# The output projection of a hybrid transformer layer in a seven-product form, with x added by accumulating transfers and two plain pairs ahead of the first MLP product

## The chip, the cores and the metric

One NeuronCore of one Trainium2 chip. The metric is the device time of one launch in microseconds. Names of engines as in the profile: PE is TensorE (matmuls; PEld its weight loads), DVE VectorE, ACT ScalarE, POOL GpSimd, SP SyncE, which only issues transfers. Transfers that add to what lies at their destination ("accumulating") are issued by POOL in this kernel.

## The reference, cut to what matters

x has 512 tokens of 2048 features in float32, the hidden layer of the MLP 8192.

```python
def reference(x, g_mix, w_in, ..., w_oa, w_ob, w_out, g_ff, w_ff1, w_ff2):
    h = rms_norm(x, g_mix)
    q, k, v, u, v_sg, gate_a, gate_b = split(h @ w_in)
    y_a = stick_breaking_attention(q, k, v) @ w_oa
    y_b = spatial_gating(gelu(u), gelu(v_sg)) @ w_ob
    merged = sigmoid(gate_a) * y_a + sigmoid(gate_b) * y_b
    x = x + merged @ w_out
    h2 = rms_norm(x, g_ff)
    return x + square(relu(h2 @ w_ff1)) @ w_ff2
```

## The kernel before

Tokens are four blocks of 128 (`NTB`), features 16 tiles of 128 (`KT`), column pieces 512 wide (`W`). Every large product is made from float32 in three matmuls: each factor is split into a high part, rounded by ACT, and a low part, the difference made by DVE (`split_to`, L113 and L114), and `mm3` multiplies high by high, high by low and low by high (L72, L73, L74). `weight` (L99 and L101) does the same for a piece of a weight that SP loaded, 1024 elements to a partition; the split pieces go through a ring of six tiles, that is three pairs.

The stages in order of time: the input projection and attention; y_a (`by_column` over w_oa), y_b (`by_column` over w_ob) and merged (L836 on DVE, L847 on POOL); x + merged @ w_out; the first MLP product; the second MLP product. In w_out `by_token` goes over four column pieces j, and in each over eight pieces of two row tiles, with four banks of PSUM, one for each token block. x is loaded by SP into the tile `x2`, and when a column piece is done, `evac_x` adds the bank to it on DVE (L868), squares it on ACT for the norm (L869) and writes it to `kept`, from which it is added again at the end (L1086). In the steps of the next column piece `turned` transposes x2 on PE (L884), multiplies by gain and norm on DVE (L888) and splits the result, the factors of the first MLP product.

The MLP products use a form with seven products of half size in place of eight (`NAMES`: y11, y21, m7, m6, y22, m4, m5); sums and differences of the quarters are the factors (`factor`, L251, for activations, `Sums` for weights). The first MLP product has 32 pairs of hidden tiles; the first one (`PLAIN`) is made without that form by `plain_pair`, while the factors m7, m6, m5, m4 of the input are made, the other 31 by `strassen_pair`. The second one goes over eight blocks of `strassen_tokens`, each with seven products of two units (i = 0, 1) of 12 matmuls. `Sums` holds six raw tiles for each unit: the quarters w11, w12, w21, w22, and two sums. `a` = w11 + w21 is the factor of m7, `c` = a + w22 that of m6; then c becomes c + w12, the factor of y22; w21 gets w22 added by an accumulating transfer of POOL (L188) for m5.

The order on each engine is set by a scheduler with a timing model of its own, within the order of the data. Each engine, POOL among them, then takes its instructions strictly in that order. What is run beside the matmuls is queued in `behind`, one entry for each `step()`; `at_steps` puts functions at numbered steps (`steps[n]`), counted from the start of w_oa: w_oa has 0 to 15, w_ob 16 to 31. Raw tiles come from pools: a block's transfer into a tile waits until the block before has read it.

Of the kernel before, what the change touches and what calls it, by code (L numbers as in the profile page):

```python
# [35 lines left out]
def tile_hybrid_layer(ctx: ExitStack, tc: tile.TileContext, x, g_mix, w_in, g_q, g_k, ln_g, ln_b,  # L36
# [816 lines left out]

    EARLY = 6

    def first_factors(k):
        for name, sign, pool in (("m7", -1.0, long if k < LONG - KT // 2 else slots), ("m6", None, slots)):
            factor(hs, x2T[2 * k:2 * k + 2], k, name, sign, pool)
# [4 lines left out]
    kept = dram.tile([NTB, D // W, P, W], F32, name="kept")
    ss2 = const.tile([P, NTB, 4], F32, name="ss2")
    for j in range(D // W):
        def evac_x(tb, o):
# [1 line left out]
            nc.vector.tensor_tensor(out=t, in0=o, in1=t, op=ALU.add)  # L868
            nc.scalar.activation(out=o, in_=t, func=AF.Square, accum_out=ss2[:, tb, j:j + 1])  # L869
# [11 lines left out]
        def turned(c, j=j):  # L881
            t = aux("x2T")
            for tb in range(NTB):
                nc.tensor.transpose(out=t[:, tb * P:(tb + 1) * P], in_=x2[tb, j][:, c * P:(c + 1) * P],  # L884
                                    identity=ident)
            k = j * 4 + c
            keep = slot("x2T")
            nc.vector.scalar_tensor_tensor(out=keep, in0=t, scalar=gT2[:, k:k + 1], in1=rstd_b,  # L888
                                           op0=ALU.mult, op1=ALU.mult)
            x2T.append(keep)  # L890
            for half in range(2):
                name = "y" + "12"[k % 2] + "12"[half]
                hs[name, k // 2] = halves(keep[:, half * HS:(half + 1) * HS],
                                          long if name == "y11" else slots)

        behind.extend([lambda c=c, turned=turned: turned(c) for c in range(4)])
        if j == D // W - 2:
            behind.extend([lambda k=k: (first_factors(k), first_factors(k + 1)) for k in range(0, EARLY, 2)])
    flush()
# [220 lines left out]
```

## Time and profile before

| what | us |
|---|---|
| median of 3 runs (lowest, highest) | 2416.53 (2415.04, 2416.75) |
| the profiled execution's own time | 2416.75 |
| its span | 2415.0 |
| w_oa and w_ob, 795.0 to 984.4 | 189.4 |
| w_out, 984.4 to 1164.6 | 180.2 |
| the plain pair, 1164.6 to 1190.2 | 25.6 |
| five Strassen pairs, 1258.3 to 1355.2 | 96.9 |

In rows of a timeline the first number is the start, the second the length, in us. In groups the count stands behind x, then the busy time in us and the mean of one in ns, then the idle time of the engine ahead of them with what ended it. Matmuls are pipelined, so that a row's length is more than the interval between two; the interval is taken from the starts of rows a known number of matmuls apart.

### The profile page before, as it was taken

The numbers are of one execution on the slowest core, as the hardware profiler recorded it, in microseconds if no ns is written. First come the engines' busy times: TensorE is split into PE (matmuls) and PEld (weight loads), VectorE is DVE, ScalarE is ACT, GpSimd is POOL, SyncE is SP. The second block draws the span as 40 slices with busy tenths as digits, with TensorE's granted clock in tenths as the row PEclk, the third lists the DMA queues.
The fourth block names the chain that finished last, engine by engine and source line by source line (L and its number), as shares of the span: only waits on it lengthen the run. The fifth ranks groups of instructions, "written<-read, shape, count | busy, mean of one in ns | idle before, by whom it ended". The sixth has DMA issues, their size and how long they took to land.

```text
span 2415.0 us, 34398 instructions
## 1 busy us (share of the span) xinstructions
PE 2401.7 (99%) x12452; PEld 2058.2 (85%) x12452; DVE 1879.3 (78%) x2555; ACT 1283.5 (53%) x1977; POOL 475.0 (20%) x586
## 2 busy tenths in 40 slices
PE   9999999999999999999999999999999999999999
PEld 8888888888888878888988888888888788888887
DVE  5576887777778554445788888888888898989987
ACT  5335666666666323233577777777765443333333
POOL 0101222222223322100000000000025334322210
PEclk9999999999999999999999999999999999999999
DMA  5557887878888843443488888888887999877753
GB/s 184 196 161 162 170 176 173 187 170 180 174 180 194 329 149 131 131 148 125 102 229 225 239 232 232 225 231 232 226 271 262 315 274 323 252 219 210 233 183 96
DMA packets 511770, 490.94 MB, mean 203 GB/s; under 512 B 20657, under 2 KB 401649, under 8 KB 511601
## 3 DMA queue, kind: packets, MB, share of 16 engines
q1 hardware_dynamic: 385232, 336.68, 43.7%
q0 software_dynamic: 126080, 151.55, 29.8%
q8 instruction: 98, 1.61, 0.3%
q10 hardware_dynamic: 288, 0.52, 0.1%
q14 instruction: 72, 0.58, 0.1%
HBM read 397.97 MB, written 89.65 MB: 202 GB/s over the span
## 4 chain that ended last, share of the span: by engine, by line
PE 94%; DMA 2%; DVE 2%; ACT 1%; issue 1%; POOL 0%; SPq 0%; DVEq 0%; ACTq 0%
PE q L223 18%; PE fork L223 13%; PE q L226 9%; PE q L73 7%; PE q L74 7%; PE q L72 7%; PE fork L226 7%; PE xo L72 2%; PE xo L74 2%; PE xo L73 2%; DMA w_raw<-in_w_ff_dram 1%; PE v L72 1%; PE v L73 1%; PE v L74 1%; PE vg L72 1%; PE vg L73 1%
## 5 line engine op out<-in xcount | busy, mean ns | idle before, releaser
L113 ACT CAST w_hi<-w_raw 128x1024 fp32r<-128x1024 f32 (+1 forms) x639 | 671.3, 1051 | 726.1 <-PE q L73 325.5
L114 DVE TENSOR_TENSOR w_lo<-w_raw,w_hi 128x1024 fp32r<-128x1024 f32 (+1 forms) x639 | 777.8, 1218 | 181.8 <-ACT w_hi L113 166.0
L223 PE MATMUL q<-ys,w_hi 128*128 128x512 f32 x1664 | 419.0, 393 | 1.7 <-ACT fork L231 1.7
L73 PE MATMUL q<-w_lo,ys 128*128 128x512 f32 x896 | 349.3, 390 | 2.7 <-DVE w_lo L114 2.5
L74 PE MATMUL q<-w_hi,ys 128*128 128x512 f32 x896 | 348.7, 389 | 0.0
L223 PEld LDWEIGHTS q<-ys,w_hi 128*128 128x128 f32 x1664 | 299.4, 189 | 56.1 <-ACT fork L231 2.1
L72 PE MATMUL q<-w_hi,ys 128*128 128x512 f32 x896 | 312.8, 389 | 0.2 <-DVE total L1062 0.2
L188 POOL DMA_DIRECT2D w_raw<-in_w_ff_dram x58 | 80.9, 1395 | 892.8 <-ACT act L1000 230.9
L223 PE MATMUL fork<-ys,w_hi 128*128 128x512 f32 x968 | 242.2, 392 | 0.0
L226 PEld LDWEIGHTS q<-ys,w_lo 128*128 128x128 f32 x1664 | 225.2, 190 | 14.3
L226 PE MATMUL q<-ys,w_lo 128*128 128x256 f32 x1664 | 232.1, 282 | 0.0
L101 DVE TENSOR_TENSOR w_lo<-w_raw,w_hi 128x1024 fp32r<-128x1024 f32 x99 | 124.8, 1260 | 136.4 <-ACT w_hi L99 131.5
L99 ACT CAST w_hi<-w_raw 128x1024 fp32r<-128x1024 f32 x99 | 104.1, 1051 | 227.5 <-issue 95.6
L223 PEld LDWEIGHTS fork<-ys,w_hi 128*128 128x128 f32 x968 | 175.9, 189 | 32.6
L73 PEld LDWEIGHTS q<-w_lo,ys 128*128 128x128 f32 x896 | 168.2, 188 | 40.1 <-DVE w_lo L114 5.2
L72 PEld LDWEIGHTS q<-w_hi,ys 128*128 128x128 f32 x896 | 168.1, 188 | 35.6 <-issue 0.6
L74 PEld LDWEIGHTS q<-w_hi,ys 128*128 128x128 f32 x896 | 168.2, 188 | 34.7
L1008 POOL DMA_DIRECT2D ys<-store x224 | 126.7, 578 | 182.1 <-PE q L74 115.9
L226 PEld LDWEIGHTS fork<-ys,w_lo 128*128 128x128 f32 x968 | 132.0, 190 | 9.4
L186 DVE TENSOR_TENSOR w_raw<-w_raw 128x1024 f32<-128x1024 f32 x91 | 111.1, 1222 | 31.3 <-DVE act L285 12.1
L1062 DVE SCALAR_TENSOR_TENSOR total<-q,plus,total 128x512 f32<-128x512 f32 x180 | 132.0, 744 | 4.2 <-PE q L74 4.1
L226 PE MATMUL fork<-ys,w_lo 128*128 128x256 f32 x968 | 135.0, 282 | 0.0
(263 smaller groups left out, 3887.0 us busy)
## 6 DMA issues: line engine op xcount, KB each, us to landing
w_raw<-in_w_ff_dram SPq DMA_DIRECT2D x256, 512.0 KB, 5.7
w_raw<-in_w_in_dram SPq DMA_DIRECT2D x143, 512.0 KB, 5.4
ys<-store POOLq DMA_DIRECT2D x224, 256.0 KB, 6.5
w_raw<-in_w_ff_dram POOLq DMA_DIRECT2D x58, 512.0 KB, 6.9
w_raw<-in_w_in_dram POOLq DMA_DIRECT2D x56, 512.0 KB, 6.5
store<-ys_hi SPq DMA_DIRECT2D x90, 256.0 KB, 5.3
store<-ys_lo SPq DMA_DIRECT2D x90, 256.0 KB, 5.2
w_raw<-in_w_out_dram SPq DMA_DIRECT2D x32, 512.0 KB, 4.1
```

Source lines behind the costliest of these rows:

```text
L72: nc.tensor.matmul(o, lhsT=lh[0], rhs=rh[0], start=start, stop=False, **kw)
L73: nc.tensor.matmul(o, lhsT=lh[0], rhs=rh[1], start=False, stop=False, **kw)
L74: nc.tensor.matmul(o, lhsT=lh[1], rhs=rh[0], start=False, stop=stop, **kw)
L99: nc.scalar.copy(out=hi, in_=raw)
L101: nc.vector.tensor_tensor(out=lo, in0=raw, in1=f32(hi), op=ALU.subtract)
L113: nc.scalar.copy(out=hi, in_=src)
L114: state["lo"] = nc.vector.tensor_tensor(out=lo, in0=src, in1=f32(hi), op=ALU.subtract)
L186: nc.vector.tensor_tensor(out=self.a, in0=self.w11, in1=self.w21, op=ALU.add)
L223: nc.tensor.matmul(o, lhsT=hi[:, k, :], rhs=rhs[name][k], start=name in ("y11", "m7") and k == 0, stop=False, skip_group_check=True)
L226: nc.tensor.matmul(o[:, :HS], lhsT=lo[:, k, :], rhs=rhs[name][k][:, :HS], start=False, stop=k == KH - 1, skip_group_check=True)
L1008: nc.gpsimd.dma_start(out=f32(t), in_=store[f][HELD.index(name), p])
L1062: nc.vector.scalar_tensor_tensor(out=a, in0=o, scalar=part, in1=a, op0=ALU.mult, op1=ALU.add)
```

## The change

w_out is made by `strassen_tokens` in four blocks (f, g): f is a half of the row tiles, g a half of the columns, in the order (0,0), (0,1), (1,0), (1,1). The factors of merged (`ms`) are made in steps of w_ob and w_out. `evac_x` copies a first product into `x2` on ACT and adds or subtracts the later ones on DVE (L949 in the changed kernel); in the blocks with f = 1 finished tiles are written to `kept`, squared (L954) and scaled by the first norm's `rstd` (L955) on ACT; `turned` transposes them (L912), and ACT multiplies by the gain (L919). x is added to `x2` by 16 accumulating transfers of POOL (L962) in the blocks (0,1) and (1,0). With `by_dma` the weight sums come from transfers: `a` is loaded as w11 a second time by SP (L184), and POOL adds w21 to it (L321); POOL adds w12 to `c` (L205). In the last block the order of products is y11, m7, m6, m5, y22, m4, y21. Two plain pairs open the first MLP product, the first with its row tiles in the order 0, 4, 12, 8. The pool `long` is closed after w_oa and opened again after w_out; between them lies a pool of six raw tiles.

```diff
-        def __init__(self, blocks, tiles, loaded=True, twice=False):
-            self.blocks, self.loaded, self.twice = blocks, loaded, twice
+        def __init__(self, blocks, tiles, loaded=True, twice=False, given=False):
+            self.blocks, self.loaded, self.twice, self.given = blocks, loaded, twice, given
...
         def loads(self):
-            for t, hc in ((self.w11, (0, 0)), (self.w12, (1, 0)), (self.w21, (0, 1)), (self.w22, (1, 1))):
+            order = [(self.w11, (0, 0)), (self.w12, (1, 0)), (self.w21, (0, 1)), (self.w22, (1, 1))]
+            if self.given:
+                order.insert(2, (self.a, (0, 0)))
+            for t, hc in order:
                 self.load = state["load"] = nc.sync.dma_start(out=t, in_=self.blocks[hc])
                 yield
         def parts(self, name):
             if name == "m7":
-                nc.vector.tensor_tensor(out=self.a, in0=self.w11, in1=self.w21, op=ALU.add)
+                if not self.given:
+                    nc.vector.tensor_tensor(out=self.a, in0=self.w11, in1=self.w21, op=ALU.add)
                 if self.loaded:
                     state["sum"] = nc.gpsimd.dma_start(out=self.w21, in_=self.blocks[1, 1], accum_op=ALU.add)
...
-    def plain_pair(wap, c0, ys, name):
+    def plain_pair(wap, c0, ys, name, turn=(0, 4, 8, 12)):
         o = [acc(name) for _ in range(2)]
-        for kt in range(0, KT, 4):
+        for kt in turn:
...
-    def strassen_tokens(wap, r0, c0, lhs, evac, between, loaded=True, after=None, last=False):
+    def strassen_tokens(wap, r0, c0, lhs, evac, between, loaded=True, after=None, last=False, by_dma=False):
...
-                           loaded))
+                           loaded, by_dma, by_dma))
         collections.deque(zip(*[w.loads() for w in ws]), 0)
+        if by_dma:
+            for w in ws:
+                nc.gpsimd.dma_start(out=w.a, in_=w.blocks[0, 1], accum_op=ALU.add)
...
     for half in range(2):
-        steps[1 + 3 * half].append(lambda half=half: let(lambda: fetch_mix(half)))
+        steps[1 + 5 * half].append(lambda half=half: let(lambda: fetch_mix(half)))
         for i in range(2):
-            steps[3 + i + 4 * half].append(lambda half=half, i=i: split_mix(half, (2 * i, 2 * i + 1)))
+            steps[3 + i + 5 * half].append(lambda half=half, i=i: split_mix(half, (2 * i, 2 * i + 1)))
...
+    def split_merged(k, names=("y11", "y21", "y22")):
+        for name in names:
+            half = int(name[2]) - 1
+            ms[name, k] = halves(mt[2 * k + int(name[1]) - 1][:, half * HS:(half + 1) * HS])
+    def merged_factors(k, *names):
+        for name in names:
+            factor(ms, mt[2 * k:2 * k + 2], k, name)
+    OB, XO, FF = 16, 32, 60
...
+    for n, what in ((21, (0, 0)), (22, (0, 1)), (23, (1, 0)), (24, (1, 1)), (25, (3, 1)), (26, (2, 1)), (27, (3, 0)),
+                    (27, (2, 0))):
+        steps[XO + n].append(lambda what=what: turned(*what))
+    for k in range(KT // 2):
+        steps[FF + k].append(lambda k=k: input_factors(k, ("m7", "m6", "m5", "m4")))
...
-    mT = []
+    first.close()
+    second = ExitStack()
+    state["more"] = second.enter_context(tc.tile_pool(name="more1", bufs=6))
+    mt, ms = [], {}
...
-            mT.append(split(m, "mT", pool=long if len(mT) >= KT - 4 else slots))
+            mt.append(m)
...
-    for j in range(D // W):
-        def evac_x(tb, o):
-            t = x2[tb, j]
-            nc.vector.tensor_tensor(out=t, in0=o, in1=t, op=ALU.add)
-            nc.scalar.activation(out=o, in_=t, func=AF.Square, accum_out=ss2[:, tb, j:j + 1])
-            nc.sync.dma_start(out=kept[tb, j], in_=t)
-        ref = state["load"]
-        with tc.issue_after(ref.ins):
-            for tb in range(NTB):
-                t = slot("x2")
-                nc.sync.dma_start(out=t, in_=x[tb * P:(tb + 1) * P, j * W:(j + 1) * W])
-                x2[tb, j] = t
-        by_token(w_out[0], j * W, lambda k, tb: [part[:, tb * P:(tb + 1) * P] for part in mT[k]], KT, evac_x, "xo",
-                 turn=KT - 4 if j == D // W - 1 else 0)
...
+    takes = {"y11": [(0, 0, ALU.add)], "y21": [(0, 0, ALU.add)], "m7": [(1, 1, ALU.add)],
+             "m6": [(0, 1, ALU.subtract)], "y22": [(1, 0, ALU.add)], "m4": [(0, 1, ALU.add)],
+             "m5": [(1, 1, ALU.subtract), (1, 0, ALU.add)]}
+    done = ({"y21": [(0, 0)], "m4": [(0, 1)], "m5": [(1, 1), (1, 0)]},
+            {"m5": [(1, 1)], "y22": [(1, 0)], "m4": [(0, 1)], "y21": [(0, 0)]})
...
+                nc.scalar.activation(out=keep, in_=t[:, i * HS:(i + 1) * HS], func=AF.Copy, scale=gT2[:, k:k + 1])
...
+    for f in range(2):
+        for g in range(2):
+            def evac_x(name, t, o):
+                for half, c, op in takes[name]:
+                    key = 2 * half + t, 2 * g + c
+                    if key not in x2:
+                        x2[key] = slot("x2")
+                        nc.scalar.activation(out=x2[key], in_=o, func=AF.Copy, scale=1.0 if op == ALU.add else -1.0)
+                    else:
+                        nc.vector.tensor_tensor(out=x2[key], in0=x2[key], in1=o, op=op)
+                for half, c in done[g].get(name, []) if f else []:
+                    tb, j = 2 * half + t, 2 * g + c
+                    nc.sync.dma_start(out=kept[tb, j], in_=x2[tb, j])
+                    xs = x2s[tb, j] = slot("xs")
+                    nc.scalar.activation(out=xs, in_=x2[tb, j], func=AF.Square, accum_out=ss2[:, tb, j:j + 1])
+                    nc.scalar.activation(out=xs, in_=x2[tb, j], func=AF.Copy, scale=rstd[:, tb:tb + 1])
+            def between_x(name):
+                if f != g:
+                    i = NAMES.index(name)
+                    for n in (i, len(NAMES)) if i == len(NAMES) - 1 else (i,):
+                        tb, j = n % NTB, 2 * (1 - g) + n // NTB
+                        nc.gpsimd.dma_start(out=x2[tb, j], in_=x[tb * P:(tb + 1) * P, j * W:(j + 1) * W],
+                                            accum_op=ALU.add)
+            strassen_tokens(w_out[0], f * CHUNK * 2 * P, g * 2 * W, Merged(f), evac_x, between_x, last=f == 1 and g == 1,
+                            by_dma=True)
+    second.close()
+    third = ExitStack()
+    long = third.enter_context(tc.tile_pool(name="long2", bufs=LONG))
...
-    PLAIN = 1
...
+    PLAIN = 2
     for p in range(PLAIN):
-        o = plain_pair(w_ff1[0], p * 2 * P, hs, "f1")
+        o = plain_pair(w_ff1[0], p * 2 * P, hs, "f1", (0, 4, 8, 12) if p else (0, 4, 12, 8))
```

In the changed kernel functions stand later: L192 is the accumulating transfer into w21 that was L188, L890 the addition on POOL that was L847.

POOL's queue, from the last additions of merged on. Before, up to the first transfers of the first MLP product:

```order
L847 TENSOR_TENSOR merged_9389<-merged_9389,merged_a_8761 128x512
L847 TENSOR_TENSOR merged_9396<-merged_9396,merged_a_8763 128x512
L188 DMA w_raw_11047<-in_w_ff1_dram 128x8x128
L378 TENSOR_TENSOR rstd2_10720<-ms2_10717,mhalf_113 128x4
L188 DMA w_raw_11222<-in_w_ff1_dram 128x8x128
```

After, from the middle of block (0,1) of w_out; w_raw_9788 and w_raw_9794 are `c` of this block's two units, w_raw_10113 and w_raw_10119 are `a` of the next block's:

```order
L962 DMA x2_9608<-in_x_dram 128x512
L962 DMA x2_9699<-in_x_dram 128x512
L321 DMA w_raw_10113<-in_w_out_dram 128x2x512
L962 DMA x2_9841<-in_x_dram 128x512
L962 DMA x2_9843<-in_x_dram 128x512
L321 DMA w_raw_10119<-in_w_out_dram 128x2x512
L205 DMA w_raw_9788<-in_w_out_dram 128x2x512
L205 DMA w_raw_9794<-in_w_out_dram 128x2x512
L192 DMA w_raw_10111<-in_w_out_dram 128x2x512
L192 DMA w_raw_10117<-in_w_out_dram 128x2x512
```

Where POOL had nothing between merged and the MLP, the transfers into this block's `c` now stand behind those into the next block's `a` and two of x. In block (0,0) the order is L321, two L962, L205, L321, L205; in (1,0) both L321 stand directly ahead of both L205.

DVE in block (0,1), around the weight pieces of m6 and y22:

```order
L949 TENSOR_TENSOR x2_9841<-x2_9841,q_9854 128x512
L949 TENSOR_TENSOR x2_9843<-x2_9843,q_9855 128x512
L114 TENSOR_TENSOR w_lo_9942<-w_raw_9788,w_hi_9941 128x1024
L114 TENSOR_TENSOR w_lo_9960<-w_raw_9794,w_hi_9959 128x1024
L114 TENSOR_TENSOR w_lo_9992<-w_raw_9788,w_hi_9991 128x1024
L114 TENSOR_TENSOR ys_9982<-merged_9298,ys_9982 128x256
```

The tile w_raw_9788 is split for m6, gets w12 by the transfer L205, and is split again two pieces later for y22, with no addition on DVE between.

DVE where w_out ends and the first plain pair begins. Before, x2 of the last column piece and the pieces of the plain pair, w_lo_10741 and w_lo_10811:

```order
L114 TENSOR_TENSOR ys_10620<-x2T_10477,ys_10620 128x256
L251 TENSOR_TENSOR x2T_10477<-x2T_10477 128x256
L101 TENSOR_TENSOR w_lo_10741<-w_raw_10737,w_hi_10739 128x1024
L101 TENSOR_TENSOR w_lo_10811<-w_raw_10807,w_hi_10809 128x1024
L868 TENSOR_TENSOR x2_10301<-xo_10309,x2_10301 128x512
L868 TENSOR_TENSOR x2_10303<-xo_10310,x2_10303 128x512
```

After, with w_lo_11005 as the first plain piece:

```order
L114 TENSOR_TENSOR w_lo_10894<-w_raw_10450,w_hi_10893 128x1024
L949 TENSOR_TENSOR x2_9976<-x2_9976,q_10533 128x512
L114 TENSOR_TENSOR ys_10786<-x2T_10784,ys_10786 128x256
L949 TENSOR_TENSOR x2_9978<-x2_9978,q_10534 128x512
L117 SCALAR_TENSOR_TENSOR ys_11056<-x2T_10513,ys_11056 128x256
L101 TENSOR_TENSOR w_lo_11005<-w_raw_11001,w_hi_11003 128x1024
```

Two weight pieces of the plain pair were split ahead of the last evacuations; now the first stands behind the last two evacuations and two splits.

More of the change, by code (lines that the diff above doesn't have):

```diff
@@ L263, in plain_pair @@
                         mm3(o[c][:, half * HS:(half + 1) * HS], a, sides(y),
-                            kt + k + half == 0, kt + k == KT - 1, skip_group_check=True)
+                            kt + k + half == turn[0], kt + k == turn[-1] + 3, skip_group_check=True)
             step()
@@ L847, in evac_b @@
             nc.gpsimd.tensor_tensor(out=m, in0=m, in1=merged_a[j * 4 + c], op=ALU.add)
-            mT.append(split(m, "mT", pool=long if len(mT) >= KT - 4 else slots))
+            mt.append(m)
         by_column(w_ob[0], j * W, lambda k: sT[k], SGW // P, evac_b, "yb")
         ahead.popleft()
[L854 to L858, printed above, removed]
@@ L860, in tile_hybrid_layer @@
-    x2 = {}
-    x2T = []
-    hs = {}
+    NEAR = 4
+    x2, x2T, hs = {}, {}, {}
+    x2s = {}
     kept = dram.tile([NTB, D // W, P, W], F32, name="kept")
     ss2 = const.tile([P, NTB, 4], F32, name="ss2")
-    for j in range(D // W):
-        def evac_x(tb, o):
-            t = x2[tb, j]
-            nc.vector.tensor_tensor(out=t, in0=o, in1=t, op=ALU.add)
-            nc.scalar.activation(out=o, in_=t, func=AF.Square, accum_out=ss2[:, tb, j:j + 1])
-            nc.sync.dma_start(out=kept[tb, j], in_=t)
-        ref = state["load"]
-        with tc.issue_after(ref.ins):
-            for tb in range(NTB):
-                t = slot("x2")
-                nc.sync.dma_start(out=t, in_=x[tb * P:(tb + 1) * P, j * W:(j + 1) * W])
-                x2[tb, j] = t
-        by_token(w_out[0], j * W, lambda k, tb: [part[:, tb * P:(tb + 1) * P] for part in mT[k]], KT, evac_x, "xo",
-                 turn=KT - 4 if j == D // W - 1 else 0)
-        def turned(c, j=j):
-            t = aux("x2T")
[L883 to L898, printed above, removed]
@@ L899, in tile_hybrid_layer, with turned @@
-    flush()
+    takes = {"y11": [(0, 0, ALU.add)], "y21": [(0, 0, ALU.add)], "m7": [(1, 1, ALU.add)],
[3 more added lines that the diff above has]
+            {"m5": [(1, 1)], "y22": [(1, 0)], "m4": [(0, 1)], "y21": [(0, 0)]})
+    def turned(j, half):
+        for c in (0, 2):
+            t = aux("x2T")
+            for i in range(2):
+                for b in range(2):
+                    nc.tensor.transpose(out=t[:, (2 * i + b) * P:(2 * i + b + 1) * P],
+                                        in_=x2s[2 * half + b, j][:, (c + i) * P:(c + i + 1) * P], identity=ident)
+            for i in range(2):
+                k = j * 4 + c + i
+                if k not in x2T:
+                    x2T[k] = slot("x2T")
+                keep = x2T[k][:, half * HS:(half + 1) * HS]
+                nc.scalar.activation(out=keep, in_=t[:, i * HS:(i + 1) * HS], func=AF.Copy, scale=gT2[:, k:k + 1])
+                name = "y" + "12"[i] + "12"[half]
+                hs[name, k // 2] = halves(keep)
@@ new lines, in input_factors, with __init__, __getitem__ @@
+    def input_factors(k, names):
+        act = [x2T[2 * k], x2T[2 * k + 1]]
+        for name in names:
+            pool = long if name == "m7" or name == "m6" and k < NEAR else slots
+            factor(hs, act, k, name, -1.0 if name in ("m7", "m4") else None, pool)
+    CHUNK = 4
+    class Merged:
+        def __init__(self, f):
+            self.f = f
+        def __getitem__(self, name):
+            return [sides(ms[name, self.f * CHUNK + k]) for k in range(CHUNK)]
+    for f in range(2):
[23 more added lines that the diff above has]
+                            by_dma=True)
@@ L1028, in tile_hybrid_layer @@
         lhs.update({name: fetch(0, name) for name in NAMES[2:4]})
-    first.close()
+    third.close()
     state["more"] = ctx.enter_context(tc.tile_pool(name="more", bufs=6))
-    takes = {"y11": [(0, 0, ALU.add)], "y21": [(0, 0, ALU.add)], "m7": [(1, 1, ALU.add)],
-             "m6": [(0, 1, ALU.subtract)], "y22": [(1, 0, ALU.add)], "m4": [(0, 1, ALU.add)],
-             "m5": [(1, 1, ALU.subtract), (1, 0, ALU.add)]}
-    done = ({"y21": [(0, 0)], "m4": [(0, 1)], "m5": [(1, 1), (1, 0)]},
-            {"m5": [(1, 1)], "y22": [(1, 0)], "m4": [(0, 1)], "y21": [(0, 0)]})
     total = {}
```

22 lines of the change are left out of this document (16 added, 6 removed).

## Prediction, made before the changed kernel had run

> **What bounds the kernel now.** I read the page from the top: the busy times, then the chain that ended last.
>
> ```profile
> span 2415.0 us, 34398 instructions
> PE 2401.7 (99%) x12452; PEld 2058.2 (85%) x12452; DVE 1879.3 (78%) x2555; ACT 1283.5 (53%) x1977; POOL 475.0 (20%) x586
> PE 94%; DMA 2%; DVE 2%; ACT 1%; issue 1%; POOL 0%; SPq 0%; DVEq 0%; ACTq 0%
> ```
>
> TensorE is busy for 99% of the span and makes 94% of the chain. A matmul that goes saves its full issue interval; everything else matters only where it makes TensorE wait. The table of stretches gives the stages: w_ob, w_out, the plain pair, five Strassen pairs, most of the second MLP product. The columns are length, busy time of PE, PEld, DVE, ACT and POOL (with counts), clock, DMA share, GB/s.
>
> ```profile
> 897.40:984.40 87.00, 87.00 (x385) 72.07 (x384) 43.23 (x49) 25.27 (x30) 24.07 (x28) 1.00 0.39 132
> 984.40:1164.60 180.20, 180.20 (x818) 148.88 (x817) 83.06 (x124) 57.78 (x100) 4.34 (x3) 1.00 0.41 134
> 1164.60:1190.20 25.60, 25.60 (x213) 25.44 (x212) 22.98 (x52) 14.96 (x38) 2.68 (x2) 1.00 0.39 94
> 1258.30:1355.20 96.90, 96.90 (x559) 85.41 (x558) 86.56 (x125) 70.29 (x116) 7.75 (x5) 1.00 0.86 227
> 1960.00:2400.00 440.00, 439.79 (x1940) 363.85 (x1939) 396.91 (x415) 169.86 (x161) 106.67 (x158) 1.00 0.74 220
> ```
>
> TensorE never pauses in w_out (180.20 of 180.20), at the full clock, with VectorE at 46%. The waits of TensorE from 780 to 1260 us are one group, in w_oa:
>
> ```profile
> PE ya L72 <- DVE merged_a L836: 2.9, 2, 2.5
> ```
>
> So nothing that the change takes from VectorE, ScalarE or the SP queue in w_out can save time. It saves by matmuls alone, and it can lose by new waits.
>
> **The change, part by part. (1) Matmuls.** The interval of w_out's matmuls, from two rows 82 matmuls apart, and four transposes with the matmul behind them:
>
> ```profile
> 1056.20 0.39 PE L73 MATMUL xo<-w_lo,mT_hi 128*128 128x512 f32 x1
> 1074.79 0.39 PE L74 MATMUL xo<-w_hi,mT_lo 128*128 128x512 f32 x1
> 1045.49 0.60 PE L884 MATMUL x2T<-ident,x 128*128 128x128 f32 x4
> 1045.85 0.47 PE L72 MATMUL xo<-w_hi,mT_hi 128*128 128x512 f32 x1
> L72 PE MATMUL xo<-w_hi,mT_hi 128*128 128x512 f32 x256 | 100.1, 393 | 0.0
> ```
>
> (1074.79 − 1056.20) / 82 = 0.2267 us. Before: 3 × 256 = 768 matmuls. After: 4 blocks × 7 products × 24 = 672, same shape. The 64 transposes stay (0.09 us each). 96 × 0.2267 = **−21.8 us**.
>
> **(2) A second plain pair.** Two rows 120 matmuls apart in the plain pair; the ReLU of a Strassen pair and of the fifth one behind it:
>
> ```profile
> 1172.34 0.28 PE L74 MATMUL f<-ys,w_lo 128*128 128x256 f32 x1
> 1186.74 0.28 PE L74 MATMUL f<-ys,w_lo 128*128 128x256 f32 x1
> 1258.26 0.63 ACT L1000 ACTIVATE act<-act 128x512 f32<-128x512 f32 x1
> 1355.19 0.63 ACT L1000 ACTIVATE act<-act 128x512 f32<-128x512 f32 x1
> ```
>
> Plain: 192 matmuls × 14.40/120 = 23.04 us. Strassen: 96.93/5 = 19.39 us. One pair changes kind: **+3.65 us**. Net so far −18.1 us.
>
> **(3) VectorE and ScalarE work, hidden or not.** Unit times:
>
> ```profile
> L251 DVE TENSOR_TENSOR x2T<-x2T 128x256 f32<-128x256 f32 x32 | 12.6, 419 | 0.4
> L114 DVE TENSOR_TENSOR ys<-x2T,ys 128x256 fp32r<-128x256 f32 x48 | 18.4, 417 | 0.9 <-ACT ys L113 0.9
> L113 ACT CAST ys<-x2T 128x256 fp32r<-128x256 f32 x48 | 17.2, 402 | 11.0 <-DVE x2T L888 6.7 <-DVE x2T L251 4.3
> L868 DVE TENSOR_TENSOR x<-xo,x 128x512 f32<-128x512 f32 x16 | 11.0, 689 | 5.5 <-PE xo L74 5.3
> L869 ACT ACTIVATE xo<-x 128x512 f32<-128x512 f32 x16 | 9.6, 599 | 10.1 <-DVE x L868 10.1
> L114 DVE TENSOR_TENSOR w_lo<-w_raw,w_hi 128x1024 fp32r<-128x1024 f32 x162 | 197.7, 1221 | 40.6 <-ACT w_hi L113 36.8
> L113 ACT CAST w_hi<-w_raw 128x1024 fp32r<-128x1024 f32 x161 | 169.9, 1055 | 268.6 <-PE q L73 258.9 <-DMA w_raw<-in_w_ff_dram 4.9 <-PE q L74 1.9
> ```
>
> VectorE in w_out after: 56 w_lo pieces × 1.22, 48 evacuations × 0.69, 16 factors of merged × 0.84, 40 splits × 0.42 = 131 us of 152. ScalarE: 56 casts × 1.05, 48 copies, squares and scalings × 0.60, 32 gain multiplications and 56 casts × 0.40 = 123 of 152. The Strassen rows above run with VectorE at 89% and no pause, so on average both fit: cost 0. In w_ob the new splits and factors (16 × 0.42 + 16 × 0.84 − 12.5 for the mT splits that go) raise VectorE from 43 to 51 of 87 us: 0. In the two plain pairs 32 factors and 8 pieces make 37 us of 46: 0. If this cover is gone, the price is a wait at one place, the seam (5).
>
> **(4) The y22 wait.** This is the term that I expect to cost. The second MLP product shows how such blocks run: a unit of 12 matmuls (one half-product) uses one piece pair, and the ring has three.
>
> ```profile
> 2002.36 1.06 ACT L113 CAST w_hi<-w_raw 128x1024 fp32r<-128x1024 f32 x1 [1.67 <-PE q L73]
> 2048.64 1.05 ACT L113 CAST w_hi<-w_raw 128x1024 fp32r<-128x1024 f32 x1 [1.66 <-PE q L73]
> w_raw<-in_w_ff_dram SPq DMA_DIRECT2D x86, 512.0 KB, 4.5
> w_raw<-in_w_ff_dram POOLq DMA_DIRECT2D x22, 512.0 KB, 6.2
> total<-kept POOLq DMA_DIRECT2D x16, 256.0 KB, 9.4
> 1964.83 1.79 POOL L1086 DMA_DIRECT2D total<-kept  x2 [7.48 <-DVE total L1062]
> L188 POOL DMA_DIRECT2D w_raw<-in_w_ff_dram x22: 1179/1224/1343, 1980.5 to 2363.3; - x22
> DMA to landing us min/median/max: 5.5/6.2/9.5
> ```
>
> 17 units in 46.28 us are 2.72 us each, and a cast waits for TensorE to finish the unit three back. An accumulating 512 KB transfer lands 6.2 us after its issue and holds POOL for 1.22; a 256 KB one holds it for 0.89.
>
> Let a block start at 0, units 0 to 13. Unit n's split ends at 2.72 × (n − 2) + 1.05 + 1.22. The sums `a` (m7, units 4 and 5) are split by 7.7 and 10.4; only then may the next block's load into each start, landing 4.5 later, at 12.2 and 14.9. Unit 6 (m6) is split at 13.2, and only then may `c` take its accumulate (L205 of the changed kernel). Unit 8 (y22) starts at 21.8 and needs its low part by 22.2, so the accumulate has to land by 19.9. Issued at 13.2 it lands at 19.4: no wait. But in POOL's order (shown with the change) the next block's L321, which waits for the load just named, and two x transfers stand ahead of it:
> - block (0,0): L321 12.2 to 13.4, x to 15.2, L205 lands at 21.4, split at 23.7: wait 1.5
> - block (0,1): L321, x to 15.2, second L321 to 16.4, lands 22.6, split 24.9: 2.7
> - block (1,0): second L321 14.9 to 16.1, lands 22.3, split 24.6: 2.4
> - block (1,1): no next block, and m5 lies between m6 and y22: 0
>
> Sum **+6.6 us**. TensorE runs in order, so such a wait isn't won back. Before, this sum was a VectorE addition and had no such path; so a gain here is excluded. The bounds: 0 at the fastest nearby landing, SP's in w_out, 3.9; and 20.1 if each accumulate takes the slowest one's 9.5 and each load 5.7:
>
> ```profile
> w_raw<-in_w_out_dram SPq DMA_DIRECT2D x24, 512.0 KB, 3.9
> w_raw<-in_w_ff_dram SPq DMA_DIRECT2D x256, 512.0 KB, 5.7
> ```
>
> (9.5 − 6.2 and 5.7 − 4.5, together 4.5 more per block, × 3). I take 4.5 and 6.2, since the changed stage moves about 36 MB in 160 us, 225 GB/s, like that stage's 220.
>
> For accumulating transfers the Trainium skill, "DMA: Bandwidth & Descriptors", section "Anatomy of one DMA — SWDGE (gpsimd) path", gives about 2.0 us plus bytes / 436,000: an estimate of 3.2 us for 512 KB, by which no wait would arise and the sum would be 6.6 us lower. The rows disagree: 22 such transfers took 5.5 us at least. I keep the rows.
>
> **(5) The seam.** Behind the last unit TensorE has 8 transposes (0.7 us) and 4 matmuls on w_hi (0.5), then needs the first plain piece's w_lo. VectorE has, ahead of it (order shown with the change), two evacuations and two splits, 2 × (0.69 + 0.42), then that piece, 1.22: 3.4 us. **+2.1 us**; before there was no wait here. Bounds: 0, if the low part is made ahead of the evacuations; 4.3, if one more such group of 2.2 us has piled up. I take the order as printed. Behind the seam the Strassen pairs are untouched: 0.
>
> The other edits: x leaves 16 SP loads for 16 POOL transfers, each ahead of L205 of the block before the one that reads its tile; their POOL time is in (4). The gating loads of w_oa move by one and two steps, beside POOL at 28% in w_ob: 0, between −2.9 (the one wait there) and +2.7 (a unit).
>
> **Sum.** −21.8 + 3.65 + 6.6 + 2.1 = −9.4 us. Durations are from the execution whose own time is 2416.75 us (span 2415.0), 0.2 above the median of the runs. 2416.75 − 9.4 = **2407.4 us**.
>
> **The rivals.**
> - *No y22 wait.* The accumulates land like SP's loads, in 3.9 us: block (0,1) would split by 22.6, 0.4 late, and 0.6 earlier loads take that off. Only the seam is left: −18.1 + 2.1, **2400.8 us**, 2398.7 without it. For it: SP's 3.9 in this very stage. Against it: 5.5 at the least on POOL's queue. By the formula of the Trainium skill cited under (4) the result would be this one too. Chance 0.15.
> - *The gain is eaten.* Loads 5.7, as on the page, and accumulates 7.0, as in the first MLP product:
>
> ```profile
> w_raw<-in_w_ff_dram POOLq DMA_DIRECT2D x28, 512.0 KB, 7.0
> ```
>
>  2.0 more in three blocks, and the seam at 4.3: −18.1 + 12.6 + 4.3, **2415.5 us**. For it: the stage gets as busy as that one. Chance 0.17.
> - *Slower: POOL's queue is late.* L205 stands behind the 256 KB accumulates of x, whose kind took 9.4 us above while the median 512 KB one took 6.2. If L205 lands at 9.5 and loads at 5.7, the y22 waits are 20.1, the seam 4.3: +6.3, **2423.0 us**. It decides from waits above 18.1 + 4.8 = 22.9 us. Against it: those rows were issued in a crowd of fetches that this stage lacks. Chance 0.12.
> - *The change doesn't do what it says*: 96 fewer matmuls stand in the program's order. Chance 0.01, time as before.
>
> **How the numbers follow.** The forecast has 0.55, on its own 2402 to 2412. A measurement of this kernel can tell 0.2% from no change, 4.8 us: 2411.7 and 2421.4 are the bounds. Faster: 0.55 + 0.15 = 0.70. Same: 0.17 + 0.01 = 0.18. Slower: 0.12. The range takes in the first two rivals, each with the runs' spread of 1.7 us: 2398.7 − 1.7 = 2397.0 to 2415.5 + 1.7 = 2417.2.
>
> **What would show it.** (1) 672 matmuls at 0.227 us in w_out, 12 us or more off its 180. (2) Two plain pairs of 23.0 us, Strassen pairs still at 19.4. (4) TensorE waits on w_hi or w_lo once in each of the first three blocks, 1.5 to 2.7 us, led back to L205's landing at 6.2 us from issue; in the fourth none. (5) A wait of about 2 us at the first plain piece, on the w_lo of L101. I am wrong if waits show at other products, if SP's loads land well over 4.5 us, or if ScalarE, at 81%, ends the waits.

## The result and the profile after

The changed kernel takes 2431.45 us (median of 4 runs, 2429.15 to 2433.7), the kernel before 2416.64 beside it: a ratio of 1.0063 (95% interval 1.0045 to 1.008). It is slower by 15 us where 9 us of gain were forecast, and lies above the range. The profiled execution took 2433.7 us (span 2432.0).

The page, top and chain:

```profile
span 2432.0 us, 34714 instructions
PE 2392.4 (98%) x12436; PEld 2050.1 (84%) x12436; DVE 1943.6 (80%) x2662; ACT 1339.1 (55%) x2094; POOL 519.4 (21%) x625
PE 92%; DMA 3%; DVE 2%; ACT 1%; issue 1%; POOL 0%; SPq 0%; DVEq 0%; ACTq 0%; POOLq 0%
```

TensorE is busy for 9 us less than before, and the span is 17 us longer: 26 us more in which it does nothing. The waits of TensorE from 780 to 1260 us (total, times, longest) say where:

```profile
PE q L72 <- ACT w_hi L113: 23.5, 3, 11.5
PE ya L72 <- DVE merged_a L876: 1.7, 2, 1.3
PE q L72 <- DVE x L949: 0.8, 1, 0.8
PE f L74 <- DVE w_lo L101: 0.6, 1, 0.6
PE x2T L912 <- ACT xs L955: 0.2, 1, 0.2
```

The three waits on w_hi in TensorE's timeline, with rows around the first (start, length, the idle time ahead in brackets):

```profile
1006.46 0.39 PE L74 MATMUL q<-w_hi,ys 128*128 128x512 f32 x1
1010.58 1.22 PE L72 MATMUL q<-w_hi,ys 128*128 128x512 f32 x2 [3.74 <-ACT w_hi L113]
1011.84 0.80 PE L73 MATMUL q<-w_lo,ys 128*128 128x512 f32 x1
1012.43 0.63 PE L74 MATMUL q<-w_hi,ys 128*128 128x512 f32 x1
...
1015.85 0.63 PE L74 MATMUL q<-w_hi,ys 128*128 128x512 f32 x1
...
1063.94 1.22 PE L72 MATMUL q<-w_hi,ys 128*128 128x512 f32 x2 [11.45 <-ACT w_hi L113]
...
1112.57 1.22 PE L72 MATMUL q<-w_hi,ys 128*128 128x512 f32 x2 [8.29 <-ACT w_hi L113]
```

w_out begins at 984.92, and unit 8 of the first block is due 8 × 2.72 = 21.8 us later, at 1006.7: the first wait is y22's. The others are y22's of blocks (0,1) and (1,0) (due at 1052.3 and 1104.3); block (1,1) has none. Behind a wait the matmuls are slow: from 1012.43 to 1015.85 eight intervals take 3.42 us, 0.43 each, where 0.227 is full speed. The table of stretches has it in the clock (second number from the right but two):

```profile
984.40:1022.00 37.60, 33.82 (x136) 26.74 (x135) 21.94 (x35) 19.28 (x31) 12.42 (x11) 0.91 0.73 163
1022.00:1065.00 43.00, 31.55 (x135) 24.95 (x134) 22.85 (x33) 15.15 (x21) 12.89 (x13) 0.91 0.93 212
1065.00:1110.00 45.00, 39.25 (x167) 31.96 (x166) 28.12 (x36) 19.25 (x29) 12.61 (x12) 0.96 0.94 223
...
1009.68:1016.51 6.83, 5.89 (x13) 4.20 (x14) 2.10 (x2) 3.29 (x6) 0.14 (x1) 0.50 0.78 181
1057.47:1067.71 10.24, 3.73 (x8) 2.53 (x9) 3.24 (x5) 4.53 (x7) 0.00 (x0) 0.50 0.90 189
1108.67:1115.49 6.82, 2.92 (x9) 2.42 (x10) 2.82 (x4) 2.52 (x3) 0.00 (x0) 0.50 0.72 138
```

Each row ends with the granted clock, the share of the DMA engines' time, and GB/s. The clock, 1.00 in all of w_out before, is 0.91 to 0.96 as a mean over the first three rows. It is 0.50 in the three stretches of the last rows: each begins within a wait and reaches 2.9 to 5.9 us past its end. And the DMA engines are busy for 0.93 and 0.94 in the second and third row, where w_out had 0.41 and the second MLP product, from which the landing times were taken, 0.74.

**Where the 17.0 us of span come from**, by landmarks of TensorE's timeline: 3.05 lie ahead of w_oa (this execution was the slowest of the four); w_oa to the first Strassen pair takes 427.42 us instead of 395.08, +32.34; 30 Strassen pairs take 590.52 instead of 606.43 for 31, −15.91; the second product −2.48. The +32.34 are made of −21.76 and +23.04 (the matmuls), 25.1 of waits in w_out and at the seam, −2.8 in w_oa and w_ob, and what is left, 8.8 us. Of these, **7.5 us are slow matmuls directly behind the three waits** (3.5, 2.3 and 1.7, by the starts of the rows against 0.227 us a matmul and 0.09 a transpose); the other 1.3 us weren't traced.

POOL's timeline at the three places:

```profile
996.86 1.19 POOL L321 DMA_DIRECT2D w_raw<-in_w_out_dram  x1 [8.31 <-DVE w_lo L114]
997.61 2.27 POOL L962 DMA_DIRECT2D x<-in_x_dram  x2
999.77 1.35 POOL L205 DMA_DIRECT2D w_raw<-in_w_out_dram  x1
...
1048.85 1.20 POOL L321 DMA_DIRECT2D w_raw<-in_w_out_dram  x1 [11.70 <-DMA w_raw<-in_w_out_dram]
1049.57 2.30 POOL L962 DMA_DIRECT2D x<-in_x_dram  x2
1050.67 2.44 POOL L321 DMA_DIRECT2D w_raw<-in_w_out_dram  x1
1051.39 4.21 POOL L205 DMA_DIRECT2D w_raw<-in_w_out_dram  x2
...
1099.58 2.48 POOL L321 DMA_DIRECT2D w_raw<-in_w_out_dram  x2 [11.57 <-DVE x L949]
1101.59 2.94 POOL L205 DMA_DIRECT2D w_raw<-in_w_out_dram  x2
```

and ScalarE's casts of y22, which start when `c` has landed:

```profile
1009.48 1.04 ACT L113 CAST w_hi<-w_raw 128x1024 fp32r<-128x1024 f32 x1 [6.54 <-DMA w_raw<-in_w_out_dram]
...
1062.84 1.04 ACT L113 CAST w_hi<-w_raw 128x1024 fp32r<-128x1024 f32 x1 [15.16 <-DMA w_raw<-in_w_out_dram]
...
1111.48 1.04 ACT L113 CAST w_hi<-w_raw 128x1024 fp32r<-128x1024 f32 x1 [12.58 <-DMA w_raw<-in_w_out_dram]
```

Block by block (from a block's start, its unit 8's due time less 21.8; predicted / measured, us):

| block | last row ahead of L205 | L205 issued | to landing | wait |
|---|---|---|---|---|
| (0,0) | 13.4 / 12.7 (x) | 15.2 / 14.9 | 6.2 / 9.6 | 1.5 / 3.7 |
| (0,1) | 15.2 / 20.1 (L321) | 16.4 / 20.8 | 6.2 / 11.4 | 2.7 / 11.5 |
| (1,0) | 14.9 / 17.1 (L321) | 16.1 / 19.1 | 6.2 / 9.8 | 2.4 / 8.3 |

(In this table the first column has the start of that row; where two of a kind stand together, of their row.) In block (0,1) POOL stood idle for 11.70 us until the load into the next `a` had landed. (In (1,0) the profile names VectorE's L949 in its place.) SP's loads from 1030 to 1070 us:

```profile
  POOL w_raw L321: 11.7, 1
...
DMA to landing us min/median/max: 7.5/9.2/9.7
```

9.2 us instead of 4.5, and 9.7 for the one that L321 waited for. Meanwhile `c` was free: its m6 split on VectorE ended at 1042.0, 9.4 us ahead of L205's issue. What delayed its landing is seen in the DMA queues from 1050 to 1065 us, where SP's queue has no packet and q0, POOL's, takes all of the engines' time:

```profile
q0 software_dynamic: 1376, 2.62, 100.1%
```

Six transfers were issued there within 3.3 us, L205 as the fifth, and they land one after the other, in the order of their issue. In block (1,0), with four of 512 KB in a row, the landings lie 2.5 to 2.6 us apart (1106.3, 1108.8, 1111.4, 1113.9). So L205 paid twice for its place in POOL's queue: it was issued late, and then the transfers ahead of it had to be moved first. The groups by queue for 984 to 1164 us (packets, MB, share of 16 engines), and the issues:

```profile
q0 software_dynamic: 7744, 14.68, 47.4%
q1 hardware_dynamic: 11752, 20.04, 33.2%
...
w_raw<-in_w_out_dram SPq DMA_DIRECT2D x28, 512.0 KB, 5.9
w_raw<-in_w_out_dram POOLq DMA_DIRECT2D x20, 512.0 KB, 8.6
x<-in_x_dram POOLq DMA_DIRECT2D x16, 256.0 KB, 7.5
```

q0 holds what POOL issued, here all accumulating: 47.4 / 14.68 = 3.2% of the engines' time per MB, against 33.2 / 20.04 = 1.7% for SP's plain transfers. **An added byte costs the DMA engines about twice a copied one.** It is the addition, not POOL's queue: from 1803 to 1827 us, where POOL's only transfers are plain fetches from `store`, q0 took 19.8% for 1.68 MB. In time of all 16 engines that is 2.8 us per MB, against 3.0 for SP's plain transfers and 5.8 for the accumulating ones above.

### The profile page after: what moved, and what is told of

Its sections match the earlier page's. It is cut to its first block, busy times and chain, and to the rows that moved or that the text cites. A ratio compares the mean times of both kernels' runs of the same rounds, so it can differ in the third digit from the quotient of the medians.

```text
span 2432.0 us, 34714 instructions
## 1 busy us (share of the span) xinstructions
PE 2392.4 (98%) x12436; PEld 2050.1 (84%) x12436; DVE 1943.6 (80%) x2662; ACT 1339.1 (55%) x2094; POOL 519.4 (21%) x625
## 4 chain that ended last, share of the span: by engine, by line
PE 92%; DMA 3%; DVE 2%; ACT 1%; issue 1%; POOL 0%; SPq 0%; DVEq 0%; ACTq 0%; POOLq 0%
PE q L227 17%; PE fork L227 13%; PE q L72 9%; PE q L73 9%; PE q L74 9%; PE q L230 9%; PE fork L230 7%; DMA w_raw<-in_w_out_dram 2%; PE v L72 1%; PE v L73 1%; PE v L74 1%; PE vg L74 1%; PE vg L73 1%; PE yb L74 1%; PE yb L72 1%; PE vg L72 1%
## 5 line engine op out<-in xcount | busy, mean ns | idle before, releaser
L113 ACT CAST w_hi<-w_raw 128x1024 fp32r<-128x1024 f32 (+1 forms) x688 | 722.5, 1051 | 809.8 <-PE q L73 366.8
L114 DVE TENSOR_TENSOR w_lo<-w_raw,w_hi 128x1024 fp32r<-128x1024 f32 (+1 forms) x688 | 838.0, 1220 | 245.7 <-ACT w_hi L113 227.7
L73 PE MATMUL q<-w_lo,ys 128*128 128x512 f32 x1120 | 439.5, 392 | 0.9 <-DVE w_lo L114 0.8
L74 PE MATMUL q<-w_hi,ys 128*128 128x512 f32 x1120 | 437.4, 391 | 0.0
L72 PE MATMUL q<-w_hi,ys 128*128 128x512 f32 x1120 | 395.1, 392 | 24.5 <-ACT w_hi L113 23.5
L227 PE MATMUL q<-ys,w_hi 128*128 128x512 f32 x1632 | 411.0, 394 | 4.4 <-ACT fork L235 4.4
L72 PEld LDWEIGHTS q<-w_hi,ys 128*128 128x128 f32 x1120 | 211.1, 189 | 70.0 <-ACT w_hi L113 24.7
L73 PEld LDWEIGHTS q<-w_lo,ys 128*128 128x128 f32 x1120 | 211.4, 189 | 48.8 <-DVE w_lo L114 5.3
L74 PEld LDWEIGHTS q<-w_hi,ys 128*128 128x128 f32 x1120 | 211.4, 189 | 43.5
L192 POOL DMA_DIRECT2D w_raw<-in_w_ff_dram x57 | 79.2, 1390 | 714.3 <-ACT act L1009 162.1
L101 DVE TENSOR_TENSOR w_lo<-w_raw,w_hi 128x1024 fp32r<-128x1024 f32 x71 | 93.5, 1317 | 67.9 <-ACT w_hi L99 66.1
L99 ACT CAST w_hi<-w_raw 128x1024 fp32r<-128x1024 f32 x71 | 74.6, 1051 | 119.8 <-issue 43.7
L190 DVE TENSOR_TENSOR w_raw<-w_raw 128x1024 f32<-128x1024 f32 x90 | 110.0, 1223 | 31.1 <-DMA w_raw<-in_w_in_dram 11.3
L194 DVE TENSOR_TENSOR w_raw<-w_raw 128x1024 f32<-128x1024 f32 x98 | 119.9, 1223 | 18.0 <-DMA w_raw<-in_w_out_dram 11.0
```

Source lines behind the costliest of these rows:

```text
L72: nc.tensor.matmul(o, lhsT=lh[0], rhs=rh[0], start=start, stop=False, **kw)
L73: nc.tensor.matmul(o, lhsT=lh[0], rhs=rh[1], start=False, stop=False, **kw)
L74: nc.tensor.matmul(o, lhsT=lh[1], rhs=rh[0], start=False, stop=stop, **kw)
L101: nc.vector.tensor_tensor(out=lo, in0=raw, in1=f32(hi), op=ALU.subtract)
L113: nc.scalar.copy(out=hi, in_=src)
L114: state["lo"] = nc.vector.tensor_tensor(out=lo, in0=src, in1=f32(hi), op=ALU.subtract)
```

## The experiments

Theory: L205, behind the next block's L321 and two transfers of x in POOL's queue, lands late, and that is the loss, waits and halved clock together. Rivals: the DMA engines are so full that lateness only moves to another transfer; x's transfers are the crowd; VectorE is what ends the waits. All times are medians; the kernel before had 2416.2, 2416.7 and 2415.9 us beside the three groups of four.

**1. c by VectorE.** The transfer into `c` undone.

```diff
-                           loaded, by_dma, by_dma))
+                           loaded, False, by_dma))
```

> One part undone: c gets w12 from a VectorE addition again, not from POOL's transfer; a still comes from transfers. Theory A (the late landing of the transfer into c is the whole loss): no wait of TensorE at y22 in any block, no stretch of halved clock in w_out, 23.5 us of waits and some 8 us of slow matmuls gone: 2400 us (2398 to 2404). Rival B (the DMA engines are full, so another transfer, into a or w21, is late in its place): waits of 8 us or more at m7 or m5, 2410 to 2425. Rival C (the eight additions of 1.22 us push VectorE late): waits on w_lo, 2403 to 2408.

2406.01 us, 0.9961 of before (0.9948 to 0.9974), 25.4 us below the changed kernel, but not down to 2400. TensorE's waits from 984 to 1190 us, and VectorE's longest kind from 984 to 1140:

```profile
PE q L73 <- DVE w_lo L114: 2.7, 3, 1.5
PE q L72 <- ACT w_hi L113: 1.3, 1, 1.3
...
DVE w_raw L194 <- DMA w_raw<-in_w_out_dram: 11.8, 5, 4.3
```

The long waits at y22 are gone, so theory A holds for the bulk. But VectorE's addition for m6 (L194) stood for 11.8 us, nearly all of it on SP's loads (up to 10.5 us to landing, L321 8.9 in the median), and weight pieces behind it in VectorE's order came late. Rival B has a part: with 0.91 of the engines' time in use from 984.4 to 1098 us, lateness shows at another transfer. The time lies in the range of rival C (VectorE late by its own work), and w_lo is where C put the waits; but here VectorE itself stood and waited for loads, and experiment 9 gives it twice as many additions without harm.

**2. a by VectorE.** The other sum undone; L321 and the second load of w11 go.

```diff
-                           loaded, by_dma, by_dma))
+                           loaded, by_dma, False))
-        if by_dma:
-            for w in ws:
-                nc.gpsimd.dma_start(out=w.a, in_=w.blocks[0, 1], accum_op=ALU.add)
```

> The other part undone: a is a VectorE addition again, so the second load of w11 by SP and the transfers L321 are gone; c still gets w12 by POOL's transfer. Theory A1 (L321 stands ahead of L205 in POOL's queue and waits for its load): L205 goes right behind the split of m6, 13.2 us into a block, lands 6 to 8 us later, waits at y22 of 0 to 1.5 us, 2400 to 2405 us. Rival B (full DMA engines make L205 land after 10 us wherever it is issued): about 4 us at y22 in three blocks and slow matmuls behind them, 2412 to 2420.

2409.39 us, 0.9976 (0.9966 to 0.9985). L205 takes 7.1 us (median), 10.7 at most; TensorE waits 1.6, 3.6 and 1.6 us at y22, 6.7 in all. Between the two: without L321 the waits on w_hi fall from 23.5 to 6.7, yet the time is above the 2400 to 2405 of A1.

**3. Only the order of POOL's queue.** All transfers stay; L321 (here L322) is held behind the L205 of the block before.

```diff
             for w in ws:
-                nc.gpsimd.dma_start(out=w.a, in_=w.blocks[0, 1], accum_op=ALU.add)
+                with tc.issue_after(state["sum"].ins) if r0 or c0 else nullcontext():
+                    nc.gpsimd.dma_start(out=w.a, in_=w.blocks[0, 1], accum_op=ALU.add)
```

> Only the order of POOL's queue is changed: each block's L321 goes behind the L205 of the block before; all transfers stay. Theory A1 (queue order): L205 at 13.2 us into the block, landing at the 8.6 us median of this stage, 1.9 us of wait in each of three blocks, little time at half clock: about 2405 us (2401 to 2410). Rival B (the engines are full and the landing takes over 10 us anyway): 4 us or more per block and the clock halved behind each: 2418 to 2425.

2408.71 us, 0.9969 (0.9958 to 0.998): 22.7 us below the changed kernel, with the same bytes and the same number of transfers. POOL in block (0,1), and what TensorE waited for from 984 to 1190 us:

```profile
1035.61 1.48 POOL L205 DMA_DIRECT2D w_raw<-in_w_out_dram  x1
1037.62 1.20 POOL L205 DMA_DIRECT2D w_raw<-in_w_out_dram  x1 [0.53 <-DVE w_lo L114]
1039.17 1.19 POOL L322 DMA_DIRECT2D w_raw<-in_w_out_dram  x1 [0.36 <-issue]
...
PE q L72 <- ACT w_hi L113: 5.0, 3, 2.9
```

L205 goes as soon as `c` is split, 14 us into the block (due time of unit 8, 1043.4, less 21.8), instead of 20.8. That fits A1 (5.7 us of waits expected, 5.0 measured) and rules out that the landing alone made the loss. 9.5 us are left to the fastest kernel below (experiment 9): L205 still takes 6.7 us to land (median, 10.0 at most), and the longest wait has halved clock behind it.

**4. x left out, order as in the change.**

```diff
-                if f != g:
+                if False:
```

> The 16 transfers that add x are left out (x isn't added to the product of w_out here); the order of L321 ahead of L205 stays. Theory A1 (L321's wait for its load sets the issue of L205): the order still holds L205 back, waits of 2 to 5 us at y22 of the three blocks, 2408 to 2418 us. Rival D (the transfers of x are the crowd that makes loads and sums late): loads land in 4 to 5 us, L205 in 6 to 7, waits under 1 us, 2399 to 2403.

2419.24 us, 1.0013 (1.0003 to 1.0022): 12 us below the changed kernel. SP's loads land in 4.1 us, as D says, but L205 in 8.5, and TensorE waits 10.7 us in four places, 6.9 of it at y22 of block (1,0), the one where both L321 stand ahead of both L205. So A1 and D both hold a part, and the time lies just above A1's 2408 to 2418. It isn't clean: in block (0,1) the scheduler now put one L205 ahead of the second L321.

**5. Both: new order, x left out.** The edits of 3 and 4 together.

> L205 ahead of the next block's L321, and the 16 transfers that add x left out (x isn't added to the product of w_out here). Theory D (the crowd of x's transfers makes what is left of the waits at y22, 5.0 us with the new order alone): L205 lands in 5.5 to 6 us, waits under 1 us, no halved clock, 2400 to 2403 us. Rival (the weight transfers are crowd enough): 3 us or more of waits at y22, 2405 to 2409.

2400.68 us, 0.994 (0.9924 to 0.9957), L205 at 5.7 us (6.6 at most), 1.0 us of wait on w_hi, clock 1.0. Theory D for the remainder: order and crowd together are the loss, but for the 1.5 us that are left to experiment 9.

**6. More room behind m6.** All blocks in the last block's order of products, with the matching `done`.

```diff
-        names = ("y11", "m7", "m6", "m5", "y22", "m4", "y21") if last else NAMES
+        names = ("y11", "m7", "m6", "m5", "y22", "m4", "y21") if last or by_dma else NAMES
-                for half, c in done[g].get(name, []) if f else []:
+                for half, c in done[1].get(name, []) if f else []:
```

> All four blocks take their products in the last block's order (y11, m7, m6, m5, y22, m4, y21), so that two more units, 5.4 us, lie between m6 and y22; the scheduler then also puts L205 ahead of the next block's L321. Theory A (lateness of the transfer into c is the loss): no wait at y22, no halved clock, 2400 to 2404 us. Rival B (full DMA engines make the transfer into w21, now needed right behind m6, late in its place): waits of 3 us or more at m5, 2408 or more.

2412.99 us, 0.9987 (0.9978 to 0.9997). No wait at y22, and L205 lands in 5.5 us. But m6 now comes two units earlier, and VectorE's L194 stands on SP's loads (16.5 us, up to 10.1 to landing) with weight pieces behind it: TensorE waits 4.1, 3.2 and 2.5 us on w_lo, 9.8 in all. A miss in the number (2400 to 2404): the rival's kind of result, though at another transfer than it named.

**7 and 9. Both sums by VectorE**, run twice; x still comes by transfers. Edits 1 and 2 together.

> Both weight sums are VectorE additions again; x is still added by transfers. Theory A: no wait on a transfer; but VectorE has 16 more additions of 1.22 us, 151 of the 152 us of w_out, so waits on w_lo of 4 to 12 us: 2404 to 2412 us. Rival (VectorE's work runs ahead, into the stages beside): under 3 us of waits, 2400 to 2403.

> The kernel of ac_dve again, with more rounds, as the base of the other three: 2400.2 us (2399 to 2402), no halved clock.

2400.19 us, 0.9934 (0.9919 to 0.9949), and with more runs **2399.2 us, 0.9929 (0.9916 to 0.9941)**: 16.7 us below the kernel before, the fastest that was run. I had expected VectorE to be short; the rival, that it runs ahead, was right. Its stretch from 984.4 to 1098 us and TensorE's waits from 984 to 1190:

```profile
984.40:1098.00 113.60, 113.60 (x507) 94.07 (x505) 100.95 (x130) 65.33 (x95) 22.18 (x23) 1.00 0.73 180
...
PE q L72 <- ACT x2T L916: 0.9, 1, 0.9
PE q L72 <- ACT w_hi L113: 0.5, 1, 0.5
```

TensorE has no pause in the first three blocks, VectorE is at 89%, the clock at 1.00 and the DMA engines at 0.73.

**8. The second plain pair alone**, on the kernel before.

```diff
-    PLAIN = 1
+    PLAIN = 2
```

> The kernel before with two plain pairs in place of one, nothing else changed. The term of the sum: one pair at 23.04 instead of 19.39 us, +3.65 us, 2419.8 us (2419.2 to 2420.6). Rival (the pair's 16 more steps give the factors more room or move the queue of loads): under +2 or over +6 us.

2423.39 us, 1.0029 (1.0019 to 1.004), +6.7 us. The plain pair itself costs what the sum had: the first Strassen pair begins 48.49 us behind the first plain matmul, where it was 25.46, that is 23.03 for one pair. The rival's bound, over +6 us, was passed all the same. The rest are 3.0 us of new waits further on, in the Strassen pairs (2.3 us for 0.7) and the second product (3.9 for 2.5), and a stretch of halved clock behind one of these. The change has such waits too (3.4 us in the Strassen pairs); there a Strassen pair less gave 15.9 us, not 19.4.

**10. x by SP again, on 7.** SP loads x into x2 ahead of the first two blocks, VectorE adds the first product; L962 goes.

> As ac_dve, and x too comes without an accumulating transfer: SP loads it into x2 ahead of the first two blocks and VectorE adds or subtracts the first product, where ScalarE copied it. Theory D (x's transfers still crowd the loads of ac_dve, waits of 4 us): loads back to 4 us, and 2398 to 2400 us. Rival (16 more VectorE additions of 0.69 us, 11 us, find no room beside 140 of 156 us): waits on w_lo, 2402 to 2410 us.

2404.39 us, 0.995 (0.9935 to 0.9965): 5.2 us slower than with x's transfers. In w_out TensorE waits 3.2 us on w_hi, three times, once with the clock halved behind it. The longest idle time of ScalarE ahead of these casts is 7.23 us, ended by a sum of VectorE (L196), and VectorE works without a pause there. The additions found no room: with the sums on VectorE, x's transfers are worth having.

**11 and 12. A wait without transfers, on 7.** In block (0,1) POOL adds w12 to `c` and takes it off again, in four or six operations, ahead of y22 (the line that sets the number is left out here).

```diff
+            if name == "y22":
+                for i in range(state.pop("slow", 0)):
+                    nc.gpsimd.tensor_tensor(out=self.c, in0=self.c, in1=self.w12, op=(ALU.add, ALU.subtract)[i % 2])
```

> As ac_dve, but in block (0,1) POOL adds w12 to c and takes it off again, four operations of about 2.8 us (twice the 1.38 us of a 512-wide one), so that y22 comes late with no transfer in it. Theory G (any wait of TensorE is followed by halved clock): one wait of 5 to 6 us and 2 to 3.3 us of slow matmuls behind it, 2408.5 us (2407 to 2410). Rival (the clock was halved by the load of the transfers): the wait alone, clock 1.0, 2405.7 us (2405 to 2406.5).

> The same with six operations: one wait of 10.5 to 11.5 us. Theory G: and some 2.3 us of slow matmuls behind it, 2413.5 us (2412 to 2415.5). Rival: the wait alone, 2411.2 us (2410 to 2412), clock 1.0.

2408.09 and 2412.93 us, against 2399.2: +8.9 for a wait of 5.98 us, +13.7 for one of 10.86. TensorE and the stretch behind the wait, with four operations:

```profile
1047.71 1.22 PE L72 MATMUL q<-w_hi,ys 128*128 128x512 f32 x2 [5.98 <-ACT w_hi L113]
...
1047.50:1060.00 12.50, 12.24 (x42) 9.44 (x43) 9.60 (x10) 6.91 (x10) 2.43 (x2) 0.77 0.68 177
```

Both waits cost 2.9 us more than they last, and the clock falls to 0.77 as a mean with the DMA engines at 0.68. Theory G: the wait itself halves the clock, not the transfers; in experiment 9 they load the engines as much (0.73), with the clock at 1.00.

## Why the prediction was wrong, step by step

- **(1) and (2), matmuls: right.** In experiment 9, with hardly a wait, w_oa to the first Strassen pair takes 395.64 us (before 395.08) and there is one Strassen pair less; the span is 17.7 us shorter for 18.1 in the sum. That they agree to 0.4 us is in part luck: in that trace the Strassen pair that went gave 16.9 us, not 19.4, while w_oa and w_ob, put at 0, took 2.8 us less.
- **(3), VectorE and ScalarE hidden: right**, and with more room than I gave them: 16 further additions in experiment 9 brought no wait on VectorE into w_out.
- **(4), the y22 wait: the right place, queue and blocks, and mis-sized.** Predicted 6.6 us, measured 23.5. Two numbers in it failed, both from one choice, "I take 4.5 and 6.2, since the changed stage moves about 36 MB in 160 us, 225 GB/s, like that stage's 220". Equal GB/s was no equal load: the stage moved only 193 GB/s, but 42% of its bytes are accumulating ones at twice the engine time, and the engines went to 0.93 against 0.74. And the working let each accumulate land 6.2 us behind its own issue, whatever stood ahead of it; 512 KB ones in a row land 2.5 us apart. So L205 landed in 9.6 to 11.4 us, and the loads ahead of L321 in 9.2, which POOL's order handed on to L205. Experiments 3, 4 and 5 separate the two: the order 22.7 us, x's crowd 12, both 30.8 (they overlap).
- **A term was missing: the clock.** The sum took a wait at its length, and gave no reason for that. The three waits brought 7.5 us of slow matmuls behind them. The trace of before had it already, behind the one long wait of w_oa:

```profile
851.48 0.50 PE L72 MATMUL ya<-oT,w_hi 128*128 128x512 f32 x1 [2.52 <-DVE merged_a L836]
...
852.20 0.63 PE L74 MATMUL ya<-oT,w_lo 128*128 128x512 f32 x1
852.62 0.63 PE L72 MATMUL ya<-oT,w_hi 128*128 128x512 f32 x1
```

  0.42 us from one matmul to the next. The Trainium skill, "TensorE: Matmul & The Clock Gate", section "Part 1: The HAM clock gate (the "warmup" mystery)", states that the array falls to half its clock after an idle window of about 3.4 us and needs one busy window to come back; the waits of 3.7 us and more agree; this one of 2.52 us, shorter than the page's window, had a halved stretch too, and there the measurement decides. At this length it goes either way: in the trace of experiment 8 the same wait of 2.5 us is followed by a clock of 1.00 (851.2 to 855.0 us), as is the one of 2.50 us in experiment 6; those of 2.7 us and more in w_out and behind it all had a halved stretch, and of the shorter ones three had (1.31, 1.28 and 1.68 us, in experiments 1, 4 and 10).
- **(5), the seam: 2.1 us predicted, 0.6 measured** at the first w_lo of the plain pair, with 1.0 on other tiles in the last block.
- **Rivals.** The slower one named the cause, L205 behind other transfers in POOL's queue; at 9.5 and 5.7 us it gave 20.1 us of waits, 23.5 came. Its chance of 0.12 was too low: the row of 9.4 us for transfers of x's kind stood in the prediction, and I set it aside as a crowd "that this stage lacks". The time of the first rival (no wait, 2400.8 us) was reached in experiments 5, 7 and 9, where order and crowd, or the transfers for both sums, were taken away; its reason was not, for no 512 KB accumulate of w_out landed in 3.9 us. The estimate of 3.2 us by the Trainium skill's formula, which the page gives for transfers of GpSimd without a word on adding, is met by none of them in any run either; 5.4 us was the least.

In sum, −18.1 from the matmuls as predicted, +23.5 at y22, +8.8 left over (7.5 of it slow matmuls behind the waits), and about +3 elsewhere (seam, start of the execution, Strassen pairs, less w_oa, w_ob and the second product) give the 17.0 of the two spans.

## What to carry to other kernels

A transfer that replaces a cheap operation of an engine with room isn't free: it takes a place in an in-order issue queue, and what stands ahead of it there may wait for something that has nothing to do with it. Before costing it by a landing time from another stage, compare the share of the DMA engines, not the GB/s, count accumulating bytes twice, and add the time of the transfers ahead in the same queue. In traces like these, charge each wait of TensorE over some 2.7 us with 2 to 3 us more for the clock.

## What the runs showed of the hardware

- An accumulating transfer took about twice the DMA engine time of a plain one per byte: 3.2% against 1.7% of the engines per MB in a window of 180 us and also with x left out (experiment 5: 33.5% for 10.49 MB, 40.2% for 24.65 MB). Plain transfers of POOL took no more than SP's.
- Accumulating transfers of POOL land in the order of their issue; with almost nothing else moving, four of 512 KB in a row landed 2.5 to 2.6 us apart.
- Behind waits of 6.0 and 10.9 us with no transfer in them the matmuls ran at 0.43 us instead of 0.227 and cost 2.9 us each time; behind the three waits of the changed kernel, of 3.7, 11.5 and 8.3 us, they cost 3.5, 2.3 and 1.7. So the price doesn't grow with the wait.
- POOL's rows for these transfers overlap: the two L205 from 1051.39 on start 0.74 us apart and last 2.95 and 3.47 us, where one alone lasts 1.2. Whether the full queues cause it wasn't tried.
